# A two-block sequence model on one core: the RG-LRU's parts moved between the first SSD steps, half of w_out_2 loaded ahead of them

## The chip, the cores and the metric

One core of a Trainium2 chip runs the whole program. Its engines work side by side and wait for each other by semaphores: TensorE (PE, matrix products into PSUM), VectorE (DVE), ScalarE (ACT), GpSimd (POOL) and SyncE (SP, which here issues nearly all transfers). The metric is the device time of one execution in microseconds, the median of several runs.

## The reference

The input is one sequence of 1024 tokens with 1024 features, all in float32. The first block is a modulated mixer (retention and gated linear attention) and an MLP with squared ReLU. The second block is the one that matters here:

```python
proj = x @ w_in                        # split into z, xbc, dt, u_s5, x_rg, g_rg
y_ssd = ssd_mixer(z, xbc, dt, ...)     # conv + silu on xbc, chunked state scan, gate by silu(z), norm
y_s5  = s5_mixer(u_s5, ...)            # complex diagonal scan, gelu, GLU
y_rg  = rglru_mixer(x_rg, g_rg, ...)   # conv, gates r and i, linear scan, times gelu(g_rg)
h = layer_norm(ALPHA * x + concat([y_ssd, y_s5, y_rg]) @ w_out)
h = layer_norm(ALPHA * h + cross_attention(h, mem, ...))
h = layer_norm(ALPHA * h + squared_relu_mlp(h, ...))
```

The RG-LRU has `a = exp(-8 r softplus(-lam))` and `h_t = a_t h_(t-1) + sqrt(1 - a^2) (i xc)`.

## The kernel before

Each product of two float32 matrices is three products of "fp32r" parts: an operand is split by ACT (a cast, L82) and DVE (a subtraction, L83) into a high and a low part, and `mm3` (L109 to L116) adds high by high, high by low, low by high. Weights come in pages of 512 KB: a transfer into an S page, then the split into two pages of the tag W, H or X. A tag has a fixed number of slots (S 6, W 8, H 8, X 8, bc 3), and a page that finds none free waits until one is released.

Work is written as generators whose parts are emitted in turn. The order of emission is a priority: a scheduler, which knows the program and no measured times, lays out each engine's line, and an engine then goes through its line in order. A transfer on SP's queue that waits holds all that stand behind it.

The change lies in the second block's mixer, where these pieces meet:

- `xbc_proj` (L1256): eight steps; one step is two groups of 24 products (L114 to L116), two evictions each (L1270, L1271), a convolution of three DVE operations (L1253), tanh (L1274), a product (L1275) and the store to `s_xbc` (L1276). One load of weights serves two steps.
- `s5_mixer` (L1627): three parts.
- `rg_mixer` (L1367): part one loads the gate matrices into gw (an H page), projects and convolves x_rg; part two loads Wg, makes the gates r and gx by 16 products (L1406, L1409) and t; part three has logarithm, exponential, root and the scan (L1416 to L1423); part four multiplies with Wg (96 products), makes gelu (L1362 to L1365), the last product (L1433) and the store to `rg_od` (L1434).
- `ssd_block` (L1284): eight blocks of 128 tokens, three parts each. Part one loads the block from `s_xbc` (L1291) into an H page, transposes it (L1297, L1301), makes scores (L1303) and decays (L1320, L1321, L1322); GpSimd scales (L1311, L1312). Part two multiplies with the state and the inputs (L1328, L1332, L1335; DVE L1337 to L1344). Part three normalizes, transposes (L1353) and stores to `s_od`. `pipe` starts one block a step and runs the newer blocks' parts first.
- `out_stage` (L710): for each tile of 128 tokens loads `s_od`, `s5_od` and `rg_od` (L717), splits, and multiplies with w_out_2's eight pairs of pages, four in W (k below 4) and four in X.

Before, the first five xbc steps and part two of the RG-LRU alternate, xbc ends before part three, and all of the RG-LRU and all of w_out_2's loads are emitted ahead of the first SSD step:

```python
for g, side in ((n.s5_mixer(T), (3, 1)), (n.rg_mixer(T), (1, 3))):
    for _ in g:
        for _ in range(side[0] if side else 0):
            next(xbc, None)
        side = side[1:]
run(xbc)
n.ssd_setup()
n.wout = n.wout_load(I["w_out_2"])
```

The output stage's first tile comes behind the third SSD step (`delay(out, 3)`).

Of the kernel before, what the change touches and what calls it, by code (L numbers as in the profile page):

```python
# [17 lines left out]
NB = 8  # L18
# [1120 lines left out]
class Mix2(Mix1):  # L1139
# [227 lines left out]
    def rg_mixer(self, T):  # L1367
        nc, I = self.nc, self.I
        w = I["w_in_2"]
        gw = self.page("H").rearrange("p (z m c) -> p z m c", z=4, c=128)  # L1370
        nc.vector.memset(gw[:, 0:2], 0.0)
        for z, name in enumerate(("rg_wa_2", "rg_wx_2")):
            for h in range(4):
                r = slice(64 * (h % 2), 64 * (h % 2) + 64)
                nc.sync.dma_start(out=gw[r, z, h // 2, 64 * (h % 2):64 * (h % 2) + 64], in_=I[name][h])
        sm = self.small([128, 8], tag="rgs", bufs=1)
        nc.vector.tensor_scalar(out=sm[:, 0:2], in0=self.pvec("rg_lambda"), scalar1=-1.0, scalar2=None, op0=ALU.mult)
        self.softplus(sm[:, 0:2], 2)
        nc.vector.tensor_scalar(out=sm[:, 2:4], in0=sm[:, 0:2], scalar1=8.0, scalar2=None, op0=ALU.mult)
        nc.vector.tensor_scalar(out=sm[:, 0:2], in0=sm[:, 0:2], scalar1=-8.0, scalar2=None, op0=ALU.mult)  # L1380
        ba = self.pvec("rg_ba")
        nc.vector.tensor_scalar(out=sm[:, 6:8], in0=self.pvec("rg_bx"), scalar1=0.5, scalar2=None, op0=ALU.mult)
        self.rg_od = self.dram([128, 2, S], "rg_od")
        cw, cb = self.pvec("rg_conv_w"), self.pvec("rg_conv_b")
        Wx = self.wcols(w, 1800, 256)
        xcs = []
        for m in range(2):
            raw, xc = self.page("X"), self.page("X")
            for h in range(2):
                sl = slice(512 * h, 512 * h + 512)  # L1390
                ps = self.feat_out(T, Wx, slice(128 * m, 128 * m + 128), h)
                nc.scalar.copy(out=raw[:, sl], in_=ps)
                nc.scalar.activation(out=xc[:, sl], in_=ps, func=ACTF.Identity, scale=cw[:, 4 * m + 3:4 * m + 4],
                                     bias=cb[:, m:m + 1])
            self.conv(xc, raw, cw[:, 4 * m:4 * m + 4])
            xcs.append(xc)
        yield
        Wg = self.wcols(w, 2056, 256)
        ms = []
        for m in range(2):  # L1400
            xc = xcs[m]
            r, gx, t = self.page("H"), self.page("H"), self.page("H")
            for h in range(2):
                sl = slice(512 * h, 512 * h + 512)
                ps = self.ps("tr")
                nc.tensor.matmul(out=ps, lhsT=gw[:, 0, m], rhs=xc[:, sl], start=True, stop=True)  # L1406
                nc.scalar.activation(out=r[:, sl], in_=ps, func=ACTF.Sigmoid, bias=ba[:, m:m + 1])
                ps = self.ps("tr")
                nc.tensor.matmul(out=ps, lhsT=gw[:, 1, m], rhs=xc[:, sl], start=True, stop=True)  # L1409
                nc.scalar.activation(out=gx[:, sl], in_=ps, func=ACTF.Tanh, scale=0.5, bias=sm[:, 6 + m:7 + m])  # L1410
            nc.scalar.activation(out=t, in_=r, func=ACTF.Tanh, scale=sm[:, 2 + m:3 + m])
            nc.vector.scalar_tensor_tensor(out=gx, in0=gx, scalar=1.0, in1=xc, op0=ALU.add, op1=ALU.mult)
            ms.append((xc, r, gx, t))
        yield
        for m, (xc, r, gx, t) in enumerate(ms):
            nc.scalar.activation(out=xc, in_=t, func=ACTF.Ln, bias=1.0)  # L1416
            nc.scalar.activation(out=xc, in_=xc, func=ACTF.Exp, scale=-1.0)
            nc.scalar.activation(out=r, in_=r, func=ACTF.Exp, scale=sm[:, m:m + 1])
            nc.vector.tensor_tensor(out=t, in0=t, in1=xc, op=ALU.mult)
        for m, (xc, r, gx, t) in enumerate(ms):  # L1420
            nc.scalar.activation(out=t, in_=t, func=ACTF.Sqrt, scale=0.5)
            nc.vector.tensor_tensor(out=gx, in0=gx, in1=t, op=ALU.mult)
            nc.vector.tensor_tensor_scan(out=t, data0=r, data1=gx, initial=0.0, op0=ALU.mult, op1=ALU.add)  # L1423
        yield
        for m, (xc, r, gx, t) in enumerate(ms):
            x, q = self.page("X"), self.page("X")
            for h in range(2):
                sl = slice(512 * h, 512 * h + 512)
                ps = self.feat_out(T, Wg, slice(128 * m, 128 * m + 128), h)
                nc.scalar.activation(out=x[:, sl], in_=ps, func=ACTF.Copy, scale=0.5)  # L1430
                nc.scalar.activation(out=q[:, sl], in_=ps, func=ACTF.Square)
            self.gelu(x, q, q)
            nc.vector.tensor_tensor(out=t, in0=t, in1=q, op=ALU.mult)  # L1433
            nc.sync.dma_start(out=self.rg_od[:, m, :], in_=t)  # L1434
# [432 lines left out]
def build(tc, I, out):  # L1867
    from contextlib import ExitStack
    with ExitStack() as ctx:
        n = Mix2(tc, ctx, I, out)  # L1870
        n.modulation()
        n.kv_mem()
        def run(g):
            while True:
                try:
                    next(g)
                except StopIteration as e:
                    return e.value

        def delay(g, k):  # L1880
            for _ in range(k):
                yield
            yield from g

        norm, kv = n.first_norm(I["x"]), n.kv_proj()
        T, steps = None, [3, 0, 1, 0, 1]
        while T is None:
            n.w_eng = n.nc.gpsimd
            for _ in range(steps.pop(0) if steps else 1):
                next(kv, None)  # L1890
            n.w_eng = n.nc.vector
            T = next(norm)
        run(kv)
        def early():
            for _ in range(3):
                yield
            yield from n.mods()
            yield from n.s5_setup()
        run(n.weave(n.gla_proj(T), early(), 0.75))
        n.gla_setup()  # L1900
        run(n.weave(n.ret_proj(T), n.pipe(n.gla_block(i) for i in range(NB)), 0.3))
        n.ret_setup()
        n.gate1 = n.bcast(n.mod["gate1"][0])
        n.wout = n.wout_load(I["w_out"], n.gate1, (4, 6))
        run(n.pipe(n.ret_block(i, T) for i in range(NB)))
        T = run(n.block1_out())
        T = n.block1_mlp(T)
        n.dt_proj(T)
        xbc = n.xbc_proj(T)
        for g, side in ((n.s5_mixer(T), (3, 1)), (n.rg_mixer(T), (1, 3))):  # L1910
            for _ in g:
                for _ in range(side[0] if side else 0):
                    next(xbc, None)
                side = side[1:]
        run(xbc)
        n.ssd_setup()
        n.wout = n.wout_load(I["w_out_2"])
        out = n.block2_out()
        T = next(out)
        run(n.weave(n.pipe(n.ssd_block(i) for i in range(NB)), delay(out, 3)))  # L1920
        T = run(n.attention(T))
        n.block2_mlp(T)

# [85 lines left out]
```

## Time and profile before

| | us |
|---|---|
| median of 3 runs | 2644.02 (2642.16 to 2648.84) |
| profiled execution | 2643.23 |
| its span | 2641.4 |
| PE busy | 2536.1 (96%) |
| DVE busy | 1877.5 (71%) |
| ACT busy | 1165.0 (44%) |
| GpSimd busy | 240.6 (9%) |

The span is the time from the first to the last instruction in the trace; the execution's own time is 1.8 us longer. Busy times are sums over one engine's instructions, so engines overlap. The granted clock is TensorE's, as a share of 2.4 GHz. A wait is put down to the instruction whose semaphore came last. All rows are of this one execution.

### The profile page before, as it was taken

To read this page: it belongs to the slowest core of one execution; us is meant where nothing else is said; L and a number is where in the kernel's file an instruction comes from. 1 tells how busy PE (TensorE), PEld (TensorE's weight loads), DVE (VectorE), ACT (ScalarE), POOL (GpSimd) and SP (SyncE) were. 2 spreads that over 40 slices of the span, in tenths; PEclk is the share of its full clock that TensorE was granted. 3 is DMA by queue.
4 is the path that set the end of the run, shared out by engine and by line. 5 is a ranking of instruction groups with operands and counts; after the bars stand their busy time and mean duration, and the time that the engine had idled before them with its cause. 6 is when DMAs were issued, how large, how long until landed. Compare 5 with 4: busy or idle time off the path is not lost. (4 is left out here: it accounts for less than half of the span.)

```text
span 2641.4 us, 32947 instructions
## 1 busy us (share of the span) xinstructions
PE 2536.1 (96%) x12086; PEld 2061.0 (78%) x12086; DVE 1877.5 (71%) x3177; ACT 1165.0 (44%) x1834; POOL 240.6 (9%) x222
## 2 busy tenths in 40 slices
PE   7899989889999999999999998999999999999997
PEld 7586777677888888888877776778887888888886
DVE  4857666688898777647775468786557977777786
ACT  3622233344654444433553474652227444434342
POOL 4121135541000000000000003100000000000000
PEclk8899999999999999999999999999999999999999
DMA  9772433465166569966632334371102765799783
GB/s 327 254 266 100 144 104 96 132 163 167 61 215 236 192 218 330 325 193 223 209 128 85 106 102 133 118 246 40 56 17 84 271 218 193 257 339 333 269 281 106
DMA packets 255130, 484.36 MB, mean 183 GB/s; under 512 B 21604, under 2 KB 110964, under 8 KB 254968
## 3 DMA queue, kind: packets, MB, share of 16 engines
q1 hardware_dynamic: 247768, 470.59, 52.6%
q10 hardware_dynamic: 7200, 11.67, 1.2%
q8 instruction: 95, 1.56, 0.2%
q14 instruction: 67, 0.55, 0.1%
HBM read 338.80 MB, written 143.38 MB: 183 GB/s over the span
## 5 line engine op out<-in xcount | busy, mean ns | idle before, releaser
L114 PE MATMUL ps<-W,H 128*128 128x512 f32 x1088 | 424.8, 390 | 0.3 <-ACT H L82 0.2
L116 PE MATMUL ps<-W,H 128*128 128x512 f32 x1088 | 424.2, 390 | 0.0
L115 PE MATMUL ps<-W,H 128*128 128x512 f32 x1088 | 423.9, 390 | 0.0
L83 DVE TENSOR_TENSOR W<-S,W 128x1024 fp32r<-128x1024 f32 (+1 forms) x271 | 332.2, 1230 | 127.6 <-ACT W L82 126.7
L114 PE MATMUL ps<-U,W 128*128 128x512 f32 (+1 forms) x1064 | 419.4, 394 | 2.5 <-ACT W L82 2.2
L115 PE MATMUL ps<-U,W 128*128 128x512 f32 (+1 forms) x1064 | 417.4, 392 | 1.5 <-DVE U L372 1.5
L116 PE MATMUL ps<-U,W 128*128 128x512 f32 (+1 forms) x1064 | 416.1, 391 | 0.8 <-DVE W L83 0.8
L82 ACT CAST W<-S 128x1024 fp32r<-128x1024 f32 x287 | 297.0, 1042 | 241.5 <-PE ps L115 155.4
L83 DVE TENSOR_TENSOR H<-S,H 128x1024 fp32r<-128x1024 f32 x131 | 159.9, 1221 | 150.3 <-ACT H L82 145.5
L82 ACT CAST H<-S 128x1024 fp32r<-128x1024 f32 x131 | 137.5, 1050 | 279.9 <-PE ps L115 197.9
L114 PEld LDWEIGHTS ps<-W,H 128*128 128x128 f32 x1088 | 204.3, 188 | 43.5 <-DVE X L1106 0.8
L114 PEld LDWEIGHTS ps<-U,W 128*128 128x128 f32 (+1 forms) x1064 | 197.0, 185 | 51.1 <-ACT W L82 3.4
L116 PEld LDWEIGHTS ps<-W,H 128*128 128x128 f32 x1088 | 204.2, 188 | 41.8
L115 PEld LDWEIGHTS ps<-W,H 128*128 128x128 f32 x1088 | 204.3, 188 | 41.6
L115 PEld LDWEIGHTS ps<-U,W 128*128 128x128 f32 (+1 forms) x1064 | 197.2, 185 | 48.3 <-DVE U L372 4.6
L116 PEld LDWEIGHTS ps<-U,W 128*128 128x128 f32 (+1 forms) x1064 | 197.0, 185 | 45.7 <-DVE W L83 1.9
L116 PE MATMUL ps<-W,U 128*128 128x512 f32 x352 | 140.7, 400 | 5.3 <-DVE U L83 5.3
L114 PE MATMUL ps<-W,U 128*128 128x512 f32 x352 | 142.3, 404 | 2.3 <-DVE X L305 2.0
L115 PE MATMUL ps<-W,U 128*128 128x512 f32 x352 | 141.2, 401 | 0.0
L807 ACT ACTIVATE ev<-ev 128x512 f32<-128x512 f32 x104 | 65.3, 629 | 135.2 <-DVE ev L905 110.3
L116 PEld LDWEIGHTS ps<-W,U 128*128 128x128 f32 x352 | 67.5, 192 | 20.7 <-DVE U L83 6.6
L808 ACT ACTIVATE X<-ev 128x512 f32<-128x512 f32 x126 | 79.8, 634 | 3.4
(546 smaller groups left out, 4523.3 us busy)
## 6 DMA issues: line engine op xcount, KB each, us to landing
S<-mlp_h SPq DMA_DIRECT2D x112, 512.0 KB, 5.0
S<-in_w_ff SPq DMA_DIRECT2D x96, 512.0 KB, 5.2
mlp_h<-X SPq DMA_DIRECT2D x96, 512.0 KB, 3.8
S<-in_mlp_w SPq DMA_DIRECT2D x96, 512.0 KB, 5.1
mlp_w<-S SPq DMA_DIRECT2D x96, 256.0 KB, 2.8
S<-mlp_w SPq DMA_DIRECT2D x48, 512.0 KB, 4.8
S<-in_w_in SPq DMA_DIRECT2D x46, 512.0 KB, 5.4
X<-in_w_ada SPq DMA_DIRECT2D x32, 512.0 KB, 6.8
```

Of the source, the lines that this page charges most:

```text
L82: self.nc.scalar.copy(out=hi, in_=src)
L83: (lo_eng or self.nc.vector).tensor_tensor(out=lo, in0=src, in1=hi.bitcast(F32), op=ALU.subtract)
L114: mm(out=ps, lhsT=lh, rhs=rh, start=start and k == 0, stop=False)
L115: mm(out=ps, lhsT=lh, rhs=rl, start=False, stop=False)
L116: mm(out=ps, lhsT=ll, rhs=rh, start=False, stop=stop and k == n - 1)
L807: nc.scalar.activation(out=r, in_=x, func=ACTF.Relu)
L808: nc.scalar.activation(out=out, in_=r, func=ACTF.Square)
```

## The change

Wg's pages take the tag H in place of W, r and gx take X and t takes bc in place of H. The S5 part has two xbc steps behind each of its first two parts in place of three and one. The last four xbc steps stand behind part one of the RG-LRU; part two follows. Then come w_out_2's pages for k 0 to 3, SSD step 1, part three, SSD step 2, part four, SSD step 3, and w_out_2's pages for k 4 to 7. The output stage's first tile stays behind step 3 (`ssd` has then made its three steps, so the delay is no longer needed).

```diff
-        Wg = self.wcols(w, 2056, 256)
+        Wg = self.wcols(w, 2056, 256, tags="H")
...
-            r, gx, t = self.page("H"), self.page("H"), self.page("H")
+            r, gx, t = self.page("X"), self.page("X"), self.page("bc")
...
-        for g, side in ((n.s5_mixer(T), (3, 1)), (n.rg_mixer(T), (1, 3))):
-            for _ in g:
-                for _ in range(side[0] if side else 0):
-                    next(xbc, None)
-                side = side[1:]
+        for _ in n.s5_mixer(T):
+            for _ in range(2):
+                next(xbc, None)
+        rg = n.rg_mixer(T)
+        next(rg)
         run(xbc)
         n.ssd_setup()
-        n.wout = n.wout_load(I["w_out_2"])
+        next(rg)
+        n.wout = n.wout_load(I["w_out_2"], ks=(0, 2))
+        ssd = n.pipe(n.ssd_block(i) for i in range(NB))
+        next(ssd)
+        next(rg)
+        next(ssd)
+        run(rg)
+        next(ssd)
+        n.wout_load(I["w_out_2"], ks=(4, 6), out=n.wout)
         out = n.block2_out()
         T = next(out)
-        run(n.weave(n.pipe(n.ssd_block(i) for i in range(NB)), delay(out, 3)))
+        run(n.weave(ssd, out))
```

## Rows read from the trace of the kernel before

**Rows 1.** Stretches: start:end, length; each engine's busy us (instructions); clock; DMA

```profile
1495.00:1561.00 66.00, 64.52 (x262) 48.35 (x261) 31.09 (x26) 47.59 (x59) 0.00 (x0) 1.00 0.21 71
1561.00:1593.20 32.20, 31.87 (x140) 25.70 (x139) 26.39 (x21) 18.93 (x26) 0.00 (x0) 1.00 0.66 216
1593.20:1638.70 45.50, 34.81 (x180) 25.04 (x178) 42.43 (x71) 24.94 (x62) 19.61 (x15) 0.92 0.41 122
```

**Rows 2.** Waits of PE, 1593 to 1639: total us, times, longest

```profile
PE ps L1320 <- ACT half L477: 2.8, 1, 2.8
PE ps L1320 <- ACT half L1321: 1.4, 2, 0.7
PE ps L1297 <- DMA H<-s_xbc: 1.3, 1, 1.3
PE ps L116 <- DVE U L83: 1.2, 1, 1.2
```

**Rows 3.** Stretches with a lower granted clock (the third number from the end)

```profile
1604.00:1610.00 6.00, 3.81 (x13) 2.08 (x13) 6.00 (x8) 3.82 (x11) 2.41 (x3) 0.72 0.40 126
1626.00:1630.00 4.00, 4.00 (x16) 3.15 (x15) 3.13 (x7) 0.98 (x5) 3.15 (x3) 0.58 0.87 271
```

**Rows 4.** PE in order of time: start, us, instruction, wait before it

```profile
1445.41 0.50 PE L114 MATMUL ps<-U,W 128*128 128x512 f32 x1 [1.02 <-ACT W L82]
...
1544.60 1.88 PE L1320 MATMUL ps<-half,tri 128*128 128x512 f32 x4
...
1593.17 0.60 PE L1297 MATMUL ps<-ident,H 128*128 128x128 f32 x4
...
1607.39 0.85 PE L1297 MATMUL ps<-ident,H 128*128 128x128 f32 x3
```

**Rows 5.** A stretch of projection products alone

```profile
1430.00:1444.00 14.00, 14.00 (x63) 11.59 (x62) 14.00 (x12) 3.18 (x5) 0.00 (x0) 1.00 0.00 0
```

**Rows 6.** Groups of PE by line, 1495 to 1593: busy, mean ns, wait before

```profile
L1406 PE MATMUL ps<-X,H 128*128 128x512 f32 x8 | 4.2, 604 | 0.0
```

**Rows 7.** Tile bc, 1495 to 1640: ns min/median/max of each line's instructions

```profile
L1253 DVE SCALAR_TENSOR_TENSOR bc<-S,hw,bc x12: 1259/1280/1286, 1528.0 to 1579.2; 128x1023 f32<-128x1023 f32 x4, 128x1022 f32<-128x1022 f32 x4, 128x1021 f32<-128x1021 f32 x4
L1271 ACT ACTIVATE bc<-ps,hw x8: 780/788/800, 1521.7 to 1575.4; 128x512 f32<-128x512 f32 x8
L1274 ACT ACTIVATE S<-bc x5: 1040/1049/1061, 1496.3 to 1580.6; 128x1024 f32<-128x1024 f32 x5
L1275 DVE SCALAR_TENSOR_TENSOR bc<-S,bc x5: 1224/1226/1226, 1497.4 to 1581.6; 128x1024 f32<-128x1024 f32 x5
```

**Rows 8.** DMA issues, 1495 to 1640: KB each, median us to landing

```profile
H<-s_xbc SPq DMA_DIRECT2D x6, 512.0 KB, 5.3
s_xbc<-bc SPq DMA_DIRECT2D x5, 512.0 KB, 3.0
```

**Rows 9.** Groups of DVE by line, 1495 to 1639

```profile
L83 DVE TENSOR_TENSOR W<-S,W 128x1024 fp32r<-128x1024 f32 x9 | 10.8, 1220 | 3.1 <-ACT W L82 3.1
...
L1423 DVE TENSOR_TENSOR_SCAN H<-H,H 128x1024 f32<-128x1024 f32 x2 | 4.6, 2286 | 0.0
...
L1422 DVE TENSOR_TENSOR H<-H,H 128x1024 f32<-128x1024 f32 x2 | 2.4, 1222 | 2.3 <-ACT H L1421 2.3
```

**Rows 10.** DVE and GpSimd in order of time

```profile
1586.25 1.23 DVE L1365 SCALAR_TENSOR_TENSOR X<-X,X 128x1024 f32<-128x1024 f32 x1 [1.19 <-ACT X L1364]
...
1601.15 2.06 DVE L1365 SCALAR_TENSOR_TENSOR X<-X,X 128x1024 f32<-128x1024 f32 x1
...
1595.72 1.52 POOL L1311 TENSOR_TENSOR S<-H,s_dt 128x512 f32<-128x512 f32 x1 [172.09 <-ACT H L1298]
1600.64 1.49 POOL L1311 TENSOR_TENSOR S<-H,s_dt 128x512 f32<-128x512 f32 x1
```

**Rows 11.** Groups of ACT by line, 1495 to 1640: a table load

```profile
L1321 ACT ACT_TABLE_LOAD x1 | 1.3, 1283 | 0.0
```

**Rows 12.** Waits of SP's queue, 1580 to 1640

```profile
SPq L1434 <- DVE H L1307: 16.0, 1, 16.0
```

## The prediction

> **What bounds the kernel now.** I read the page's first part first: TensorE (PE) is busy 96% of the span, so a change can only give back time in which PE waits or runs at its low clock. Then the busy time by stretches around the changed lines [rows 1]. Up to 1593.2 us PE is full with the products of the xbc and RG-LRU projections: 64.52 of 66, then 31.87 of 32.2. From 1593.2 to 1638.7, where the first four SSD blocks run and no projection is left, it is busy 34.81 of 45.5. It lacks 10.69 us there, while VectorE (DVE) is busy 42.43.
>
> The waits of PE say where these lie [rows 2]. Two kinds come late, when the output stage starts: L1297 on block 4's load, 1.3, and L116 on output tile 0's split, 1.2. The other 8.2 us belong to the blocks' own chains, L1320 alone 2.8 and 1.4. In the same stretch the granted clock falls twice to its low level, 1.2 GHz [rows 3]: a mean of 0.72 over 6 us is 0.28 / 0.5 x 6 = 3.4 us low, 0.58 over 4 us again 3.4. PE had waited before each, is busy in most of both and does half the work, so each is worth 1.7 us. The pool is 10.7 + 3.4 = 14.1 us, all at the start of the SSD blocks.
>
> **The change part by part.** PE's line isn't the order of the program: four products of block 0 that need only constants ran at 1544.60, 49 us before its first transposes at 1593.17 [rows 4]. Emission is a priority, and ready work of lower priority fills in.
>
> *The S5 part, two and two xbc steps instead of three and one.* The same four steps and the same two weight loads. A step is 48 products, and 63 starts in 14 us [rows 5] make 0.226 us each, 10.8 a step. At risk is the third step's weights, for which PE waited 1.02 us at 1445 [rows 4]. They are asked for later now, but S5's second part stands ready beside them. Bounds: -1 if that wait goes, +1 if it comes once more. I take 0, since S5's chain and the weight pages stay.
>
> *xbc steps 5 to 8 directly behind the RG-LRU's first part.* 4 x 10.8 = 43 us of products, nothing added. What stood among and behind them now comes later: 16 gate products (8 of L1406 4.2, L1409 alike: 8.4 us [rows 6]) and the 96 of Wg, the gelu branch's projection (96 x 0.226 = 21.7). From the last xbc product to block 0's transposes lie L1271 0.79, three L1253 of 1.28, L1274 1.05, L1275 1.23 [rows 7], the store 3.0 and the load 5.3 [rows 8]: 15.2 us. Gates and Wg cover 30.1, so about 14.9 us of Wg are left when block 0 can start. That PE waits there all the same is bounded by 0 and, if all of Wg is queued behind the transposes, 15.2 - 8.4 = 6.8. I take 1.3, the nearest row, L1297's wait for block 4's load [rows 2].
>
> *The RG-LRU's later parts between the SSD steps.* No PE work is added. 14.9 us of Wg's products fill the 8.2 us of waits in the blocks, and the low clock that followed them, 3.4, goes too. The late 2.5 stay, as Wg is used up by then. PE's sum: 8.2 + 3.4 - 1.3 = 10.3 us back.
>
> *DVE, which is next.* Until 1561 it has done 31.09 us since 1495, and of the following 77.7 it is busy 26.39 + 42.43, so 5.8 idle before the blocks and 3.1 in them [rows 1]. Until 1561 it did two xbc steps (three L1253 and L1275, 5.07 each) and four RG-LRU products of 1.22 (two L1412, two L1419, each like L1422 [rows 9]). With the change it does three xbc steps and none of these: 5.07 - 4.88 = 0.2 more. If it never idled from then on, it would end 0.2 + 5.8 + 3.1 = 9.1 us earlier. The 5.8 can go: the gates' products, the scans (L1423 4.6), w_out_2's splits are ready in the wait for block 0. Of the 3.1, its waits for PE inside the blocks, between none and all stay, as Wg's products now share PE's line with the blocks; between the ends I take half, 1.5. DVE's sum: 0.2 + 5.8 + 1.5 = 7.5. It is below PE's 10.3 and decides.
>
> One cost stands open in it: the RG-LRU's third part (L1419, L1422, L1423: 2.4 + 2.4 + 4.6 = 9.4 us) may now run beside GpSimd's work for the SSD. L1365 took 1.23 us with GpSimd idle and 2.06 beside it [rows 10], 1.68 times. All 9.4 stretched so would cost 6.4, none 0. I take 0: GpSimd's first operation, L1311, waits for block 0's transposes (its releaser is L1298), and the 15.2 us ahead of them have room for this part. The 6.4 stay in the range.
>
> The Trainium skill, "SBUF — State Buffer", section "Who interferes with whom", says that a VectorE instruction with two SBUF inputs and a GpSimd instruction that reads SBUF exclude each other for the whole instruction. By it each of the third part's six could wait out a GpSimd instruction of 1.5 us, an estimate of 9 us in place of the 6.4. L1311's row beside L1365's shows the two at work at the same time, both long, so the trace is nearer to sharing.
>
> *ACT's table loads.* The Ln, Exp and Sqrt of part three now alternate with the SSD's Exp. A load costs 1.28 us [rows 11], and L1321, for which PE waits, had one ahead of it. Bounds: none more, or four more, 5.1. ACT is busy 24.94 us of the blocks' 45.5 and Wg covers PE, so I take 0.
>
> *Pages.* Wg moves from the W to the H pages. gw and Wg hold five of eight H, blocks 0 and 1 take four (gw's is free after the gates), and block 2 waits for Wg's last product, which the program's order asks for anyway (part four stands before step 3). r and gx take the X pages that raw has left and two more. t takes two of the three bc pages, behind xbc in priority; if it took them early, the last xbc steps would share one, and a page's life there, two evictions of 0.79, 3.84, 1.05, 1.23 and the store's 3.0, is 10.7 us, just under a step's 10.8. Cost 0, bound 2 (two steps with a wait of 1 each, as L114's [rows 4]).
>
> *w_out_2's first half before the blocks.* Four casts and four splits (4 x 1.22 [rows 9]) leave the full stretch for the wait for block 0; they are within DVE's count. The four loads stand in SP's queue behind xbc's stores, as before. The second half, behind step 3, takes X pages only as gelu frees them, as now, and such a cast held ACT, and with it L1320, for 2.8 us [rows 2]. Bound: +2.8 if this comes again uncovered; taken as 0, Wg being there.
>
> The sum is 7.5 us. The profiled execution took 2643.23 (span 2641.4): 2643.23 - 7.5 = 2635.7. The median of the three runs, 2644.02, lies 0.8 above it, so I say **2636.5**.
>
> **The rivals.** *A: the cover goes where nothing is missing.* The gates run among xbc's products, as L1320's four did; Wg alone then covers block 0's 15.2 us, and 6.5 are left against 8.2 of waits, while DVE has part three in its full stretch. Or the order by priority comes out much like today's, and the change does not what it says. 0 to 3 us come back; told as 2642.5. For it: DVE is full at 42.43 of 45.5. Against: xbc's end moves ahead of 30 us of products.
>
> *B: SP's queue, slower.* SP issues in order. The store of rg_od (L1434) already held it for DVE, 16.0 us at a time [rows 12]. Gelu now comes between steps 2 and 3, when DVE is full, and if block 2's load stands behind that store, it leaves only after it. Wg's last product comes at 1561 + 8.4 + 21.7 + two blocks' first parts, some 13 (an estimate: 34.81 us of PE in rows 1 for about four blocks, and 1.5 of them) = 1604. Eviction and gelu's chain take an estimated 9 (three DVE operations of up to 2.06 [rows 10], ACT's two at 1.05, eviction), the load 5.3: 1618. Block 2's transposes began at 1607.39 [rows 4], so they come some 11 us late with PE's cover gone: 2643.2 + 11 = 2654. It decides from the point where that store leaves later than 1609.6 (1609.6 + 5.3 = 1614.9, which is 7.5, the gain, after 1607.4) with blocks' loads behind it. Against: the store's priority is below steps 1 and 2, and block 2's load is held by Wg's pages in any case.
>
> *C: all of it comes back*, 14.1 us, since an earlier start takes along the late waits too: 2630. Against: DVE's 9.1 at best.
>
> **How the numbers follow.** A measurement of this kernel can tell a change from 0.3% on, 7.9 us: faster is below 2636.1, slower above 2652.0. The forecast has 0.56, its own range 2632 to 2641 (the stall of 2.8 or a table load or two on one side, PE's 10.3 and the -1 on the other). It straddles 2636.1: 0.31 faster, 0.25 same. A 0.22: 0.19 same, 0.03 faster. B 0.12: 0.11 slower, 0.01 same. C 0.10, faster. Together 0.44 faster, 0.45 same, 0.11 slower. The range goes from just below C to 2649, which takes in A and the 6.4 us of stretched DVE work, and leaves out most of B.
>
> **What would show it.** In the profile after: the last store of L1276 about 12 us earlier; Wg's products between the first three groups of L1297; PE short of less than 5 us from the first L1297 to the first output product; no stretch at the low clock there; DVE's idle time there not above 3 us. Wrong, if L1297 waits over 3 us for its load (order), if SP waits at L1434 with blocks' loads behind it (B), if DVE's operations of part three are as long as L1365's 2.06, or if waits behind 1638.7 grow by what the start gains.

## The result and the profile after

The changed kernel takes 2679.28 us (median of 4 runs, 2678.21 to 2680.01) against 2643.64 for the kernel before in the same session (2642.16 to 2648.84): ratio 1.0133, 95% interval 1.0121 to 1.0145, slower by 35 us. Executions of 3619 us and more (one of the kernel before, two of e15 below) are left out of all times and ratios. The forecast was 2636.5, its range ended at 2649, and slower had 0.11.

The stretches of [rows 1], here from the trace after (start:end, length; each engine's busy us with its instructions; granted clock; DMA):

```profile
1495.00:1561.00 66.00, 65.86 (x277) 51.55 (x276) 32.57 (x28) 30.05 (x41) 0.00 (x0) 1.00 0.21 70
1561.00:1593.20 32.20, 31.58 (x124) 22.62 (x122) 19.15 (x16) 18.03 (x24) 0.00 (x0) 1.00 0.47 155
1593.20:1638.70 45.50, 38.52 (x156) 28.02 (x154) 34.87 (x40) 38.96 (x54) 12.64 (x6) 0.85 0.19 57
```

Two things differ. The work is late: GpSimd, whose first operation belongs to block 0, has done 12.64 us of the blocks' work by 1638.7 where it had done 19.61. And the fourth engine column, ScalarE (ACT), is busy 30.05 where it was 47.59, and then 38.96 where it was 24.94. The prediction had watched DVE.

How late is read off one line that does the same work in both kernels, S5's L1742, first before, then after (min/median/max ns, first and last start):

```profile
L1742 PE MATMUL ps<-X,half x16: 591/592/697, 1486.7 to 1494.9; 128*128 128x512 f32 x16
```

```profile
L1742 PE MATMUL ps<-X,half x16: 592/592/697, 1511.7 to 1518.6; 128*128 128x512 f32 x16
```

25.0 us are lost before 1512, in the S5 part, which the prediction had costed at 0. The rest, some 10.6, is lost at the SSD blocks. The three longest waits of PE from 1593 to 1690 after, which answer to [rows 2]:

```profile
PE ps L182 <- ACT H L171: 5.0, 1, 5.0
PE ps L1332 <- ACT H L1298: 4.7, 2, 4.5
PE ps L1297 <- DMA H<-s_xbc: 3.1, 1, 3.1
```

L1332 and L1297 belong to the blocks and come up again under e5 to e8. L182 transposes the first output tile and waits for its layer norm (L171). The same 5.0 us stand in e2 and are gone in e8, e9, e10 and e13, but also in e5 and e6, which are no faster than e2: by itself this wait isn't the loss.

**The S5 part.** SP's queue in order of time (start, us, line), first before, then after:

```profile
1418.31 0.98 SPq L91 DMA_DIRECT2D S<-in_w_in  x2
...
1445.72 0.34 SPq L1276 DMA_DIRECT2D s_xbc<-bc  x1
1446.11 2.73 SPq L1689 DMA_DIRECT2D H<-s_K  x5
```

```profile
1446.22 0.34 SPq L1276 DMA_DIRECT2D s_xbc<-bc  x1
1446.61 1.78 SPq L1689 DMA_DIRECT2D H<-s_K  x3
1448.49 0.37 SPq L1694 DMA_DIRECT2D H<-s_P  x1
1452.62 0.34 SPq L1276 DMA_DIRECT2D s_xbc<-bc  x1
...
1453.48 2.36 SPq L91 DMA_DIRECT2D S<-in_w_in  x3
```

L91 loads weights of xbc. Before, those of the third step leave at 1418.31, ahead of the first store of xbc (L1276), for which SP then stands 25.8 us; five of S5's loads stand behind that store too, but PE has the third step's products meanwhile. After, the weights stand behind it as well and leave at 1453.48. PE has run out of xbc products by then and of S5's second part not all is there: S5's own loads (s_K, s_P) stand behind the same store. PE's waits from 1444 to 1465 after:

```profile
PE ps L1705 <- DMA H<-s_K: 5.8, 1, 5.8
PE ps L1708 <- DMA H<-s_P: 5.3, 2, 4.1
```

These 11.1 us are the smaller part. Behind the first of them the granted clock is at its low level, 1.2 GHz, for 40 us, though PE is busy without a gap for the second half. Stretches around these 40 us in the kernel before, in the one after, and in two experiments told of below (e3, e4):

```profile
1450.00:1470.00 20.00, 20.00 (x99) 15.66 (x97) 7.94 (x7) 4.54 (x6) 0.00 (x0) 1.00 0.45 140
```

```profile
1444.00:1450.00 6.00, 1.15 (x7) 0.80 (x5) 5.80 (x5) 2.21 (x3) 0.00 (x0) 1.00 0.46 131
1450.00:1470.00 20.00, 13.80 (x44) 10.47 (x44) 3.86 (x4) 3.15 (x3) 0.00 (x0) 0.51 0.50 155
1470.00:1490.00 20.00, 20.00 (x67) 15.54 (x67) 5.63 (x7) 3.12 (x5) 0.00 (x0) 0.50 0.00 0
```

```profile
1450.00:1470.00 20.00, 20.00 (x103) 15.53 (x102) 7.77 (x8) 4.54 (x6) 0.00 (x0) 1.00 0.58 183
```

```profile
1450.00:1470.00 20.00, 18.88 (x82) 14.70 (x82) 4.62 (x4) 3.15 (x3) 0.00 (x0) 0.81 0.53 161
1470.00:1490.00 20.00, 20.00 (x69) 15.65 (x68) 5.63 (x7) 3.21 (x6) 0.00 (x0) 0.51 0.00 1
```

What the low clock costs: 13.80 us at 0.51 and 20.00 at 0.50 are 6.8 + 10.0 = 16.8 us of full-speed work not done. PE's idle time after is 4.85 + 6.20 us in these rows, before it was 1.5 (6 - 4.50 between 1444 and 1450, none later). The difference is 9.5; 16.8 + 9.5 = 26.3, of which 25.0 arrive at L1742.

### The profile page after: what moved, and what is told of

The parts are those of the page before. It is cut to its first block, busy times and chain, and to the rows that moved or that the text cites. A ratio compares the mean times of both kernels' runs of the same rounds, so it can differ in the third digit from the quotient of the medians.

```text
span 2678.1 us, 32949 instructions
## 1 busy us (share of the span) xinstructions
PE 2556.4 (95%) x12086; PEld 2075.8 (78%) x12086; DVE 1877.6 (70%) x3177; ACT 1165.6 (44%) x1835; POOL 245.6 (9%) x222
## 4 chain that ended last, share of the span: by engine, by line
PE 74%; DVE 13%; ACT 4%; DMA 3%; issue 3%; POOL 2%; SPq 0%; DVEq 0%; ACTq 0%; POOLq 0%
PE ps L114 23%; PE ps L116 23%; PE ps L115 23%; DVE st L155 1%; POOL X L562 1%; DVE W L83 1%; DVE half L583 1%; DMA H<-g_qkb 1%; PE ps L182 1%; PE ps L1708 1%; PE ps L575 1%; DMA H<-r_qk 1%; DMA S<-in_xa_wk 1%; ACT H L171 1%; POOL W L83 0%
## 5 line engine op out<-in xcount | busy, mean ns | idle before, releaser
L116 PE MATMUL ps<-W,H 128*128 128x512 f32 x1088 | 424.2, 390 | 0.0
L114 PE MATMUL ps<-U,W 128*128 128x512 f32 (+1 forms) x1032 | 406.1, 394 | 0.0
L115 PE MATMUL ps<-U,W 128*128 128x512 f32 (+1 forms) x1032 | 404.6, 392 | 1.5 <-DVE U L372 1.5
L116 PE MATMUL ps<-U,W 128*128 128x512 f32 (+1 forms) x1032 | 403.8, 392 | 0.0
L116 PEld LDWEIGHTS ps<-W,H 128*128 128x128 f32 x1088 | 204.2, 188 | 41.6
L115 PEld LDWEIGHTS ps<-U,W 128*128 128x128 f32 (+1 forms) x1032 | 191.7, 186 | 45.9 <-DVE U L372 4.6
L114 PEld LDWEIGHTS ps<-U,W 128*128 128x128 f32 (+1 forms) x1032 | 191.5, 186 | 45.1 <-DVE H L437 1.5
L116 PEld LDWEIGHTS ps<-U,W 128*128 128x128 f32 (+1 forms) x1032 | 191.5, 186 | 42.6 <-DVE W L83 0.2
L116 PE MATMUL ps<-W,U 128*128 128x512 f32 x352 | 140.5, 399 | 3.9 <-DVE U L83 3.9
L116 PEld LDWEIGHTS ps<-W,U 128*128 128x128 f32 x352 | 67.3, 191 | 18.7 <-DVE U L83 4.7
```

What stands on the lines that cost most here:

```text
L114: mm(out=ps, lhsT=lh, rhs=rh, start=start and k == 0, stop=False)
L115: mm(out=ps, lhsT=lh, rhs=rl, start=False, stop=False)
L116: mm(out=ps, lhsT=ll, rhs=rh, start=False, stop=stop and k == n - 1)
```

## The experiments

Each kernel was timed beside the kernel before; ratios are to that, and 0.1% is 2.6 us.

**e1 to e4: the S5 part.** e1 is the kernel before with this one edit:

```diff
-        for g, side in ((n.s5_mixer(T), (3, 1)), (n.rg_mixer(T), (1, 3))):
+        for g, side in ((n.s5_mixer(T), (2, 2)), (n.rg_mixer(T), (1, 3))):
```

> The kernel before with the S5 part's edit alone: two and two xbc steps in place of three and one. Theory W (the weights of the third xbc step now stand behind S5's loads on SP's queue, PE has no product to fill the wait and goes on at 1.2 GHz): the S5 part gets about 23 us longer, 2667 us, and PE waits some 11 us for DMA H<-s_K and H<-s_P. Rival R (the loss lies in the RG-LRU's parts between the SSD steps, SP's or ACT's line): 2643 to 2646, no such waits.

2664.06 us, ratio 1.0078 [1.0054, 1.0101]: +21 us for this edit by itself (14 to 27 by the interval). PE's waits for s_K and s_P are there, 5.6 and 5.3 us: theory W.

e2 is the changed kernel with three steps and one:

```diff
-        for _ in n.s5_mixer(T):
-            for _ in range(2):
+        side = [3, 1]
+        for _ in n.s5_mixer(T):
+            for _ in range(side.pop(0)):
                 next(xbc, None)
```

> The changed kernel with the S5 part as before (three and one), all else as changed. Theory W: the S5 part is back to its old length, 2679 - 23 = 2656 us, and the 12 us above the kernel before that are left belong to the RG-LRU's parts between the SSD steps. Rival R: 2676 to 2679. My prediction of the other edits, without the S5 part, was 2636.

2656.20, 1.0047 [1.0032, 1.0062]: 12 us are left, which the rest of the change costs. 21 + 12 = 33 of 35.

e3 keeps two and two, but asks for the weights of the third step ahead of the second:

```diff
-            W = self.wcols(I["w_in_2"], 512 + 256 * c, 256)
+            W = nxt or self.wcols(I["w_in_2"], 512 + 256 * c, 256)
...
+                if (c, m) == (0, 1):
+                    nxt = self.wcols(I["w_in_2"], 768, 256)
```

> The changed kernel, still two and two steps, but the third step's weights are asked for ahead of the second step, so that their transfers stand ahead of S5's loads on SP's queue. Theory W (it is the place of the weights in the queue): 2656 us as with three and one. Rival W2 (it is the number of steps emitted ahead of S5's second part): 2679 us.

2652.97, 1.0032 [1.0020, 1.0044]. SP issues them at 1406.03 and the clock stays at 1.00 (third of the four fences above). So it isn't the number of steps that costs, but the place of two loads in SP's queue.

e4 puts 48 products that nothing uses ahead of S5's second part, two and two kept:

```diff
+        for h in range(2):
+            ps = self.ps()
+            for k in range(24):
+                nc.tensor.matmul(out=ps, lhsT=T[0][0][:, k % 8, 0:128], rhs=T[h][0][:, k % 8, :], start=k == 0, stop=k == 23)
```

> The changed kernel with 48 products (fp32r, 128x128 by 128x512, result unused) put ahead of S5's second part, 10.9 us of PE work that waits for no transfer. Theory C (the low clock of S5's second part follows from the wait ahead of it): the wait is filled, the second part runs at 2.4 GHz, which gives back some 16 us: 2663 us, although work is added. Rival C2 (S5's own products run at 1.2 GHz whatever was before them): 2679 to 2681 us.

2676.20, 1.0119 [1.0098, 1.0141]: hardly anything won, though the four executions differ: one took 2667.20 at a mean granted clock of 0.978, the others 2675 to 2680 at 0.973 to 0.975. The trace is of one of the latter. The filler took PE's longest wait there from 5.8 down to 1.1 us, yet the clock fell again (0.81, then 0.51; last of the four). Lost at the low clock: 18.88 x 0.19 + 20.00 x 0.49 = 13.4 us, and 48 products of 0.226 [rows 5] take 10.8. Why S5's products run at full clock before and in e3, where xbc's products stand among them, and not here, stays open.

**e5 to e8: the blocks, each made from e2.** e5 puts the RG-LRU's third part ahead of the first SSD step, e6 all its parts, e7 the two stores of rg_od behind step three. The edit of e5:

```diff
         n.wout = n.wout_load(I["w_out_2"], ks=(0, 2))
+        next(rg)
         ssd = n.pipe(n.ssd_block(i) for i in range(NB))
         next(ssd)
-        next(rg)
```

> The changed kernel with the S5 part back at three steps and one (that alone took 2656.2 us), and the RG-LRU's third part (L1416 to L1423) ahead of the first SSD step instead of between the first and the second. Theory A (ACT's line): the third part's activations and their table loads stand in front of block 1's copies, and PE waits 5.4 us for them at L1332; if they go first, that wait and the low clock behind it go: about 2650. Theory S (the order by readiness is the same either way, the loss is Wg's 48 products in one lump and what it pushes back): 2655 to 2657, L1332's wait of some 5 us still there.

2659.31, 1.0060 [1.0045, 1.0075]: not better, and above both theories' ranges. PE now waits for the same engine one block earlier, and longer; its waits from 1575 to 1600 in e5:

```profile
PE ps L1328 <- ACT half L1321: 13.0, 1, 13.0
```

Theory A had the right engine and the wrong cure: the work has to be done by ACT on either side of the first step.

> As the run before, but all parts of the RG-LRU mixer ahead of the first SSD step; xbc still ends behind its first part, Wg in the H pages, w_out_2's first half ahead of the blocks. Theory I (the interleaving with the SSD steps is the loss): 2643 to 2646, and output tile 1 no later than in the kernel before. Theory X (xbc's end ahead of the gates, or the pages, is the loss): 2654 to 2658.

2659.34, 1.0069 [1.0052, 1.0086]: theory X, 1.3 above its range. The interleaving with the steps isn't what costs; ACT is busy 34.78 us from 1560 to 1600 here too, against 25.21 before.

> As the first of these, with the third part between steps one and two, but the two stores of rg_od (L1434) behind the third SSD step, so that they stand behind block 2's load in SP's queue. Theory B (SP's queue: block 2's load waits behind a store that waits for DVE): block 2's load leaves earlier, PE's wait of 3 us at L1297 goes, 2650 to 2653. Theory H (the load waits for the H pages that Wg's last products hold): the load leaves at the same time behind those products, 2655 to 2657.

2656.89, 1.0055 [1.0040, 1.0070]: nothing. The first store still went out 0.4 us ahead of block 2's load, so the run doesn't part the theories by itself; a row of e2 does. What SP waited for at these two lines, 1608 to 1611:

```profile
SPq L1434 <- DVE bc L1433: 6.6, 1, 6.6
...
SPq L1291 <- PE ps L116: 0.2, 1, 0.2
```

After the store a load of the blocks had still to wait 0.2 us for one of Wg's last products (L116); Wg lies in the H pages that these loads need. So the store cost nothing here that the rows show.

e8 replaces Sigmoid, Ln and Sqrt of the RG-LRU by Tanh, which leaves these functions out of the computation:

```diff
...
-            nc.scalar.activation(out=xc, in_=t, func=ACTF.Ln, bias=1.0)
+            nc.scalar.activation(out=xc, in_=t, func=ACTF.Tanh, bias=1.0)
...
```

> As the kernel with the S5 part at three and one (2656.2 us), but the RG-LRU's Sigmoid, Ln and Sqrt are replaced by Tanh, which leaves these functions out of the computation; the instructions, their sizes and their order stay. Theory L (table loads): the loads of 1.28 us between these and the SSD's Exp go from ACT's line while it is full, 7 to 9 of them, and the kernel comes to 2645 to 2649. Theory S (the place of the third part's work in ACT's and DVE's line, not the loads): at most 2 us less, 2654 to 2656.

2644.16, 1.0001 [0.9992, 1.0011]: theory L, just below its range. With no table load e2's 12 us are gone. That is an upper bound for what the loads cost the change, since the run also takes away loads that the kernel before has; e10 and e11 below part the two. Their number isn't the point: from 1495 to 1720 the changed kernel and e2 have ten, the kernel before nine. Their place is. Between 1560 and 1620, where the first blocks run, the kernel before has two, then e2 nine (count; us, mean ns):

```profile
L1421 ACT ACT_TABLE_LOAD x1 | 1.3, 1283 | 0.0
L1321 ACT ACT_TABLE_LOAD x1 | 1.3, 1283 | 0.0
```

```profile
L1321 ACT ACT_TABLE_LOAD x3 | 3.8, 1283 | 0.1
L1416 ACT ACT_TABLE_LOAD x2 | 2.6, 1283 | 0.0
L1418 ACT ACT_TABLE_LOAD x2 | 2.6, 1283 | 0.0
L1407 ACT ACT_TABLE_LOAD x1 | 1.3, 1283 | 0.0
L1421 ACT ACT_TABLE_LOAD x1 | 1.3, 1283 | 0.0
```

In e2 some of them stand in ACT's line like this, ahead of the copy L1298 of block 1, for which PE (below) waits:

```profile
1583.12 1.04 ACT L1417 ACTIVATE X<-X 128x1024 f32<-128x1024 f32 x1
1584.17 1.28 ACT L1416 ACT_TABLE_LOAD   x1
1585.47 1.06 ACT L1416 ACTIVATE X<-bc 128x1024 f32<-128x1024 f32 x1
1586.54 1.28 ACT L1418 ACT_TABLE_LOAD   x1
1587.84 1.15 ACT L1418 ACTIVATE X<-X,rgs 128x1024 f32<-128x1024 f32 x1
1588.89 1.04 ACT L1417 ACTIVATE X<-X 128x1024 f32<-128x1024 f32 x1
1589.95 1.28 ACT L1421 ACT_TABLE_LOAD   x1
...
1593.15 0.57 ACT L1298 COPY H<-ps 128x512 f32<-128x512 f32 x1
```

```profile
1593.86 2.04 PE L1332 MATMUL ps<-S,H 128*128 128x256 f32 x4 [5.43 <-ACT H L1298]
```

L1416 is Ln, L1417 and L1418 are Exp, L1421 is Sqrt: a load stands at each change between them. The Trainium skill, "ScalarE: Activation LUTs", section "Table sets: the hidden batching unit", names a set that holds both, by which Ln and Exp would alternate without a load; these rows show a load each way. That the same section puts Exp and Tanh into one set agrees with e8, where no load is left from 1495 to 1720.

**e9: the gates back under xbc.** From e2: the gates behind xbc's fifth step as before, the third part ahead of the first SSD step, t in an H page; Wg and gelu stay behind step two.

```diff
...
         next(rg)
+        next(xbc)
+        next(rg)
         run(xbc)
...
-        next(rg)
...
```

> The changed kernel with the S5 part at three steps and one (2656.2 us), but the RG-LRU's gates (part two) stand behind xbc's fifth step, as in the kernel before, and its third part ahead of the first SSD step; only Wg's products and gelu lie behind step two (t in an H page, since two of the three bc pages would be missing under xbc). Theory A (the loss is ACT's work of the gates and of the third part, some 25 us with its table loads, which stood under xbc's products and now stands in front of the blocks' copies): ACT's busy time from 1520 to 1560 is back above 30 us, 2641 to 2646. Theory P (the loss is Wg in the H pages, or w_out_2's halves): 2650 to 2657.

2648.06, 1.0017 [1.0007, 1.0027]: 8 of the 12 us are gone, which lies between the two theories' ranges. ACT's busy time in two stretches, in the kernel before, e2 and e9 in turn:

```profile
1495.00:1560.00 65.00, 46.60 (x58) 1.00 0.20 67
1560.00:1600.00 40.00, 25.21 (x36) 1.00 0.60 197
```

```profile
1495.00:1560.00 65.00, 27.34 (x40) 1.00 0.26 84
1560.00:1600.00 40.00, 38.65 (x48) 0.87 0.26 91
```

```profile
1495.00:1560.00 65.00, 46.59 (x57) 1.00 0.20 67
1560.00:1600.00 40.00, 21.00 (x29) 0.96 0.39 131
```

19.3 us of ACT's work stood under PE's full line of xbc products. The change puts it behind them, where ACT is busy 38.65 of 40 us and every block needs its copies. The table loads are part of this work: e9 has two of them from 1560 to 1620, as the kernel before.

**e10, e11: the same RG-LRU through fewer tables.** The sigmoid becomes a Tanh, its half folded into scales and biases, and 1-a^2 becomes tanh(y)(1+a^2); e10 from e2, e11 from the kernel before:

```diff
...
-            nc.scalar.activation(out=xc, in_=t, func=ACTF.Ln, bias=1.0)
-            nc.scalar.activation(out=xc, in_=xc, func=ACTF.Exp, scale=-1.0)
-            nc.scalar.activation(out=r, in_=r, func=ACTF.Exp, scale=sm[:, m:m + 1])
-            nc.vector.tensor_tensor(out=t, in0=t, in1=xc, op=ALU.mult)
+            nc.scalar.activation(out=r, in_=r, func=ACTF.Exp, scale=sm[:, m:m + 1], bias=sm[:, m:m + 1])
+            nc.scalar.activation(out=xc, in_=r, func=ACTF.Square)
+            nc.vector.scalar_tensor_tensor(out=t, in0=xc, scalar=1.0, in1=t, op0=ALU.add, op1=ALU.mult)
...
```

> The kernel of 2656.2 us with the same RG-LRU computed through fewer tables: the sigmoid as a Tanh with its half folded into scales and biases, and 1-a^2 as tanh(y)(1+a^2) in place of Ln and a second Exp; only Sqrt is left, and one activation of 1.05 fewer for each of the two feature groups. Theory L: of the 12 us that the run without any table load gave back, most comes, since two or three loads are left: 2645 to 2649. Theory S: 2653 to 2657.

2646.12, 1.0014 [1.0000, 1.0027]: theory L, four table loads left from 1495 to 1720, and PE's wait of 5.4 gone.

> The kernel before with the same computation of the RG-LRU through fewer tables. There ACT does this work from 1500 to 1560, where PE is full with projections: theory L and every theory that counts on that cover: 2641 to 2643, within 0.1% of the kernel before. If ACT's line is short of time there too: 2634 to 2638.

2641.92, 0.9989 [0.9979, 0.9999]: next to nothing, as the same work has its cover there. It is the fastest version of all, by 0.1%. With fewer tables in both kernels the change costs 4.2 us by the medians (6.6 by the ratios), where e2 cost 13.8 (12.4). So the place of the loads is worth between about half and 70% of e2's loss, and the rest is something else.

**e12 to e15: w_out_2's second half.** e12 is the kernel before with the half's load behind the third step, e15 with it behind the first; e13 is e10 with it directly behind gelu, and e14 is that with e9's gates.

```diff
-        n.wout = n.wout_load(I["w_out_2"])
+        n.wout = n.wout_load(I["w_out_2"], ks=(0, 2))
...
+        n.wout_load(I["w_out_2"], ks=(4, 6), out=n.wout)
```

> The kernel before with one edit of the change alone: the second half of w_out_2 behind the third SSD step. The prediction's bounds for it: 0, or 2.8 us more if a cast holds ACT ahead of L1320 again. Theory A expects 2641 to 2646; theory P, in so far as it is this half, 2648 to 2655.

2649.88, 1.0019 [1.0009, 1.0028]: +5 us, within theory P's range. The half's casts on ACT (first fence before, second e12) come 19 to 26 us later, in the midst of the blocks' work, and the first output product's source is cast 3.4 us later (1638.48 against 1635.10):

```profile
L82 ACT CAST X<-S x4: 1045/1052/1061, 1588.9 to 1603.2; 128x1024 fp32r<-128x1024 f32 x4
```

```profile
L82 ACT CAST X<-S x4: 1030/1032/1040, 1614.8 to 1622.0; 128x1024 fp32r<-128x1024 f32 x4
```

> The change with three mendings: S5 at three steps and one, fewer tables, and now the second half of w_out_2 directly behind gelu, ahead of the third SSD step instead of behind it. Without the last it took 2646.1 us. Theory D (the half's casts and splits stand in the blocks' full stretch wherever that stretch begins; put earlier they find room while PE still has Wg's products): 2640 to 2644, and with that no slower than before. Theory N (their place within one step does not matter, or the earlier start of the blocks is given back in any case): 2645 to 2648.

2644.06, 0.9996 [0.9987, 1.0005]: theory D, at the edge of its range, and even with the kernel before. Against e10 the half's place gives 4.8 us by the ratios, 1.6 by the medians; the two intervals overlap, so this size isn't clear of the noise.

> As the run before, with the gates behind xbc's fifth step as well (2648.1 us without fewer tables and with the half behind step three). If the half is all that the gates' version has left (3.3 us over before): 2641 to 2645. If Wg in the H pages, which holds back blocks' loads (PE waited 6.2 us for them), is the rest: 2646 to 2649.

2649.13, 1.0015 [1.0006, 1.0024]: the half isn't what e9 has left. The cause that I gave for the other case fell too: PE waits 0.2 us for blocks' loads here, where e9 had 6.2, and 5.3 for DVE at L1328 in their place. What holds this version back stays open. It has no table load from 1560 to 1620 (e13 has four) and its gates back under xbc's products, and yet takes 5 us more than e13. So with few loads it wins nothing to put the gates back, and e9's gain probably came with the loads: the third part's place and t's page differ between e13 and e14 too, and no run moves the gates alone.

> The kernel before with the second half of w_out_2 behind the first SSD step instead of ahead of it (behind the third it cost 5 us). Theory D: the casts come some 10 us earlier than there, the first output product is late by 0 to 2 us, 2644 to 2647. Theory N: 2648 to 2651, as behind the third step.

2647.33, 1.0008 [0.9998, 1.0018]: between the two theories by its median, and no change that the interval shows. The first output product's source is cast at 1637.80, 2.7 us later than before, more than theory D's 2.

## Why the prediction was wrong, step by step

**S5, two and two: the step that failed most.** I took 0 with bounds of 1, because "S5's second part stands ready beside them". It doesn't: its loads, too, stand in SP's queue behind a store that waits 25.8 us for DVE. I had counted the steps and looked at PE's line, and had not followed SP's queue through the edit. Alone it costs 21 us (e1). Rival B named just this mechanism, loads behind a store that waits for DVE, at the wrong store.

**The gates' and the third part's place: the second that failed.** I gave ACT's table loads a bound of 5.1 and took 0 since "ACT is busy 24.94 us of the blocks' 45.5". That is the line as it stood before the change, without the 19.3 us that the change moves into it, which I counted for DVE and for PE and not for ACT. The row was in my first group: 47.59 busy until 1561. And "none more, or four more" asked for their number, which is one more; seven more came into the blocks' stretch with their work. Measured: 8 us by e9, 6 to 10 by e10 against e11, and 12 by e8 as an upper bound.

**The xbc part: right, but for a price that it left out.** Block 0's transposes, the first L1297, start at 1575.4 in e2 against 1593.2, and the last store of L1276 leaves at 1568.4 against 1582.9, 14.5 us earlier where 12 were foreseen. Wg's products stand between the groups of L1297, as foreseen, but 48 of them in one lump of 11.9 us, and block 2 waits behind it: PE waits 3.1 us at L1297 for its load after the change, 3.2 in e2, over the 3 that I had named as a sign of being wrong. I had seen under "Pages" that this load needs Wg's last product, and had put it at 0.

**DVE's sum, 7.5 us back, which decided the forecast: refuted.** I let DVE's idle time shrink. In e13 (rows below, third engine column) it did 3.2 us more than before from 1577.2 to 1593.2, as foreseen, but in the next 45.5 us it was busy 37.31 against 42.43: it idled 5.1 us more there, so it is not DVE's line that decides.

**PE's sum, 10.3 us back: refuted even where all else is mended.** Stretches of the kernel before, then of e13:

```profile
1577.20:1593.20 16.00, 15.79 (x70) 12.67 (x69) 12.01 (x11) 8.50 (x12) 0.00 (x0) 1.00 0.87 286
...
1638.70:1660.00 21.30, 21.30 (x96) 17.26 (x97) 11.99 (x28) 8.10 (x19) 0.81 (x1) 1.00 0.34 103
```

```profile
1577.20:1593.20 16.00, 12.37 (x65) 9.54 (x66) 15.24 (x14) 14.47 (x20) 10.61 (x6) 0.96 0.42 147
1593.20:1638.70 45.50, 41.77 (x185) 32.42 (x184) 37.31 (x63) 23.74 (x54) 8.29 (x6) 0.90 0.38 111
1638.70:1660.00 21.30, 18.07 (x84) 14.48 (x84) 13.51 (x32) 11.25 (x28) 3.86 (x3) 0.84 0.54 171
```

PE's lack of 10.69 us in the blocks [rows 1] falls to 3.73 in e13. But 3.63 stand ahead of it now and 3.23 behind, where PE had been full, and all three run at a lower mean clock. From 1577 to 1660 PE lacks 10.6 us against 10.9. Holes are filled in the blocks and stand ahead of them and behind them instead. This is read off the rows: no run moves Wg alone. The first output tile's source is cast 9.7 us earlier in e13 than before (1625.44, 1635.10), the second tile's 4.8 later (1644.69, 1639.88), so the head start is lost between the two.

**w_out_2's half:** bound 2.8, taken as 0; measured 5.0 behind the third step (e12), a term that was mis-sized.

**DVE beside GpSimd:** taken as 0, bound 6.4. The two scans of the third part took 3.06 and 3.13 us where they had taken 2.29 [rows 9], so 1.6 came, in the changed kernel and in e2. The scans, and L1312 and L1342 on GpSimd at the same time, in e2:

```profile
1594.61 6.11 DVE L1423 TENSOR_TENSOR_SCAN bc<-X,X 128x1024 f32<-128x1024 f32 x2
1595.67 2.91 POOL L1312 TENSOR_TENSOR S<-S,s_exp 128x512 f32<-128x512 f32 x1
1598.54 3.02 POOL L1342 TENSOR_TENSOR H<-H,srow 128x512 f32<-128x512 f32 x1
```

The other four operations (L1419, L1422) kept their 1.2. Both engines' records overlap and are long: in the kernel before's first five blocks L1312 takes 1.0 to 1.9 and L1342 1.0 to 2.0. Whether the engines share or take turns, as the Trainium skill's page cited in the prediction has it ("SBUF — State Buffer", "Who interferes with whom"), these rows don't tell; the 9 us estimated by that page are not seen.

**Rivals.** B was right in kind and sign, but at S5; at rg_od's store, where I had put it, SP waited 6.7 us after the change (16.0 before [rows 12]) and the blocks' loads behind it waited for Wg's page in any case. A and C, both faster, were not seen.

## What to carry to other kernels

When work moves, write down for every engine and every queue what moves with it, into which stretch, and what that queue then holds ahead of whom: here 21 us hung on two loads behind one store, and about half of another 12 or more on the table loads of an engine that is busy 44% of the span before and after. ACT's table loads were nearly free under PE's full line (e11) and not among the blocks; with fewer of them the same move cost 4 to 7 us in place of 12 to 14. Holes in the busiest engine are a gain only if what fills them isn't missing later.

## What was not expected of the hardware

After a wait of 5.8 us, and with 5.3 us more of waits among the next products, the granted clock stayed at 1.2 GHz for 40 us, 20 of which PE was busy throughout (20.00 of 20, 0.50), and came back when xbc's products ran again; in the trace of e4 a filler ahead of the same products didn't prevent it (0.51). The low clock cost more (16.8 us) than these waits (11.1).
